# Modulation vectors in unsplit fp32, the vector stationary in four column groups of the array

## The chip, the cores and the metric

The kernel runs on one NeuronCore of a Trainium2 chip. The metric is the device time of one execution in microseconds. The kernel before takes 2354.13 us (median of 3 runs, 2353.49 to 2354.79).

## The reference, cut to what matters

The program is a small diffusion transformer: a first block of two layers, and a second block of two layers, over 256 latent tokens and 256 context tokens of width 1024, all in fp32. Every layer shifts, scales and gates its tokens by modulation vectors, which are the product of one vector (for the latents) or another (for the context) with a wide weight matrix:

```python
shift, scale, gate = jnp.split(jax.nn.silu(c) @ w_mod + b_mod, 3, axis=-1)
shift_c, scale_c, gate_c = jnp.split(jax.nn.silu(c_ctx) @ w_mod + b_mod, 3, axis=-1)
hx = rmsnorm(x, g_pre) * (1 + scale[:, None]) + shift[:, None]
...
q, k, v, ga, uf, gf, zc, bc, cc, gc = split_cols(hx @ w_in, PROJ_SIZES)
...
x_new = x + gate[:, None] * rmsnorm(y, g_post)
```

`w_mod` is 1024 x 3072 for each of the two layers of the first block; the second block has `ada_w_2`, 1024 x 9216 for each of its layers. So each weight matrix of modulation is read once, for two vectors.

## The kernel before

Tokens stand feature-major in SBUF: 128 features on the partitions, 8 such tiles, 512 tokens (256 latent, 256 context) along the free dimension. A projection takes a chunk of 256 weight columns (1 MB, `[128, 8, 256]`), splits it into a high and a low part in fp32r (`wchunk`, lines 161 to 186: ScalarE casts at L184 or, for head chunks, L178, VectorE subtracts at L185 or L179), and forms each product as three fp32r products (`mm3`, L194 to L196). It accumulates over the 8 feature tiles into one of three PSUM banks named `acc` (or two named `sc`); other work uses three banks named `wk`. Raw weights land in two slots `wr`, and some `xr` more (4 in the opening, 1 in the first block); all are loaded by the SP queue. A tile scheduler orders the instructions of each engine by data and priority; casts and norms have a raised priority.

The modulation vectors are made in two ways. Those that are needed late in the second block are made on VectorE (`mods_dve`); the change does not touch them. The others, 9216 columns in all, are made on TensorE by `mods_pe`: 2048 columns of the first layer's `w_mod` in the opening, where everything waits for them; its last 1024 columns and the 3072 of the second layer's in the background of the first layer; and 3072 of `ada_w_2` in the background of the second layer. Background work is a generator that is stepped once between the tiles of a projection (`bg`, called from hooks).

A step of `mods_pe` is one chunk of 256 columns. It is loaded and split as any weight chunk; the stationary operand `cst` holds, for each of the 8 feature tiles, 128 columns of which four are not zero (high and low part of each vector, `set_cst`); and 16 fp32r products of 256 columns (L315, L316) accumulate into a `wk` bank. The first four rows of the result are copied to SBUF (L318). One step later two fp32 products with a 4 x 2 selection matrix (L305) turn them to columns, and VectorE adds the bias (L308):

```python
nc.tensor.matmul(ps[:, 0:256], self.cst[:, k], hi[:, k], start=(k == 0), stop=False)
nc.tensor.matmul(ps[:, 0:256], self.cst[:, k], lo[:, k], start=False, stop=(k == KT - 1))
```

In the opening, `first_block` loads x (transposed by L532), steps `mods_pe` eight times while the statistics of x are taken, and then makes the scale (L328) and the norm tiles of x (`apply_norm`: L408 `nu`, L410 `xh`, L411 `xl`), on which the first projections work (keys and values, then the first head chunk of queries). The context follows. In attention, each query head works with fp32r scores (L683, L684), fp32 transposes (L700) and fp32 products with the values (L706), whose outputs are 64 rows of a bank, one half for each head of a pair. Queries and keys are rotated in place in their bank (`rope`) before they are copied out.

Of the kernel before, what the change touches and what calls it, by code (L numbers as in the profile page):

```python
# [62 lines left out]
def constants():  # L63
# [21 lines left out]
    c["sel4"] = np.array([[1, 0], [1, 0], [0, 1], [0, 1]], f)  # L85
# [38 lines left out]
class Kern:  # L124
# [25 lines left out]
    def rawpool(self, n):  # L150
        """further slots for weights on their way in"""
        from contextlib import contextmanager

        @contextmanager
        def cm():
            with self.tc.tile_pool(name="rx", bufs=1, reuse_waits="tile") as rx:
                self.wx, self.rb, self.nw = (rx if n else None), n, 0
                yield
                self.wx = None
        return cm()  # L160
# [50 lines left out]
    def proj(self, chunk, cols, xs, segs, evict=None, korder=False, alloc=None, hook=None, order=None):  # L211
        """cols: functions (weights, k) -> [P, 128]; xs: (hi, lo) per k; evict(i, psum)"""
# [24 lines left out]
    def proj_first(self, tiles, xs, segs):  # L237
        """tiles: (chunk, column function, evict) triples; one segment after the other"""
        pss = [self.facc() for _ in tiles]
        both = list(zip(pss, tiles))  # L240
        for s in segs:
            # the last segment chunk by chunk, which frees the first one early
# [55 lines left out]
    def mods_pe(self, w, ncols, dst, bias, pin=0):  # L298
        nc = self.nc
        rows = []  # L300

        def columns(ch, row):
            ps2 = self.wk()
            for j in range(2):
                ins = nc.tensor.matmul(ps2[:, 2 * j:2 * j + 2], row[:, j * P:(j + 1) * P], self.sel4[0:4, :], start=True, stop=True)  # L305
                if pin and j == 0:
                    self.tc.keep_in_program_order(ins)
            nc.vector.tensor_tensor(dst[:, :, 2 * ch:2 * ch + 2], ps2[:, 0:4].rearrange("p (f v) -> p v f", v=2),  # L308
                                    bias[:, None, 2 * ch:2 * ch + 2].to_broadcast([P, 2, 2]), ALU.add)

        for ch in range(ncols // 256):
            hi, lo = self.wcols(w, ch * 256)
            ps = self.wk()
            for k in range(KT):
                nc.tensor.matmul(ps[:, 0:256], self.cst[:, k], hi[:, k], start=(k == 0), stop=False)  # L315
                nc.tensor.matmul(ps[:, 0:256], self.cst[:, k], lo[:, k], start=False, stop=(k == KT - 1))  # L316
            row = self.p1.tile([4, 256], F32, name="mrow", tag="mrow", bufs=3)
            nc.scalar.copy(row, ps[0:4, 0:256])  # L318
            rows.append((ch, row))
            if len(rows) > 1:  # L320
                columns(*rows.pop(0))
            yield
        columns(*rows.pop(0))
        yield
# [25 lines left out]
    class Stat:  # L350
# [19 lines left out]
        def columns(self, pin=False):  # L370
            """1/rms per token, tokens on partitions"""
# [19 lines left out]
        def finish(self, alloc=None, pin=False):  # L391
            """the same on every partition, tokens along the free dimension"""
# [40 lines left out]
    def run(self):  # L433
        with ExitStack() as es:
# [14 lines left out]
            with tc.tile_pool(name="p1", bufs=1) as self.p1:  # L449
# [3 lines left out]
                self.cst = self.p1.tile([P, KT, P], F32R, name="cst")  # L453
                nc.vector.memset(self.cst.bitcast(F32), 0.0)
                self.set_cst(0)
# [6 lines left out]
    def setup(self):  # L462
# [19 lines left out]
        self.sel4 = cp.tile([4, 2], F32, name="sel4")  # L482
        nc.gpsimd.dma_start(self.sel4, C["sel4"])
# [29 lines left out]
    def set_cst(self, base):  # L513
        """stationary columns [c hi, c lo, c_ctx hi, c_ctx lo]"""
        nc = self.nc
        for v in range(2):
            src = self.vec[:, base + v * 8:base + v * 8 + 8]
            hi = self.cst[:, :, 2 * v]
            nc.scalar.copy(hi, src)
            nc.vector.tensor_tensor(self.cst[:, :, 2 * v + 1], src, hi.bitcast(F32), ALU.subtract)  # L520

    def load_T(self, src, dst, stat, load=None, act=0):
        """token-major [256, 1024] in DRAM -> feature-major dst [P, KT, 256]"""
# [17 lines left out]
    def first_block(self):  # L541
# [4 lines left out]
        with self.rawpool(RI):  # L546
            for _ in self.load_T(I["x"][0], self.X, st[0], self.wload):
                pass
            for i, _ in enumerate(self.mods_pe(I["w_mod"][0, :, 0:2048], 2048, self.m1[0][:, :, 0:16], V["bmod"][:, 0:16],
                                               PM)):  # L550
# [7 lines left out]
        bga = self.mods_pe(I["w_mod"][0, :, 2048:3072], 1024, self.m1[0][:, :, 16:24], V["bmod"][:, 16:24])  # L558
        bgb = self.mods_pe(I["w_mod"][1], 3072, self.m1[1], V["bmod"][:, 24:48])

        def ada():
            self.set_cst(32)
            yield from self.mods_pe(I["ada_w_2"][0, :, 0:3072], 3072, self.m2[0][:, :, 0:24], V["adab0"][:, 0:24])
# [14 lines left out]
    def fb_layer(self, l, stats, bga, bgb, AB):  # L578
# [28 lines left out]
        # a head's queries and keys: [hi; lo] against [hi; hi], and hi against lo  # L607
# [40 lines left out]
        def softmax(pss, width, E, h):  # L648
            """rows of the two query tiles; E <- normalised weights"""
# [141 lines left out]
        if l == 0:  # L791
            # the segments apart: the tiles of x are ready before those of the context
# [16 lines left out]
        else:  # L809
            # x first, its statistics come before the context's  # L810
# [51 lines left out]
        # merge  # L862
# [6 lines left out]
        # out projection and post norm  # L869
# [40 lines left out]
    def second_block(self):  # L910
# [36 lines left out]
        with tc.tile_pool(name="fin", bufs=1, reuse_waits="tile") as fp:  # L947
            # tokens end up on partitions, so that 1/rms goes in last
# [128 lines left out]
    def tokproj(self, chunk, xn, tts, evict):  # L1077
        """token-major product: out[tokens, 256 columns]"""
# [678 lines left out]
```

## Time and profile before

| what | value |
|---|---|
| median of 3 runs | 2354.13 us (2353.49 to 2354.79) |
| span of the profiled execution | 2352.5 us |
| TensorE products, busy | 2287.0 us (97%), 13429 records |
| weight loads of TensorE, busy | 1968.5 us (84%) |
| VectorE, busy | 1631.1 us (69%) |
| ScalarE, busy | 969.5 us (41%) |
| data moved | 327.31 MB, 139 GB/s over the span |
| share of the last chain: TensorE | 53%, and 24% issue |

The profiled execution's own time is its span, 2352.5 us; the median of the runs stands 1.6 us above it. TensorE's products are pipelined: a product's duration reaches past the start of the next one, so that the distance between two starts, not the duration, is what a product takes of the engine. An fp32 product runs as two passes and leaves two records in the trace, an fp32r product one.

### The profile page before, as it was taken

To read this page: it belongs to the slowest core of one execution; us is meant where nothing else is said; L and a number is where in the kernel's file an instruction comes from. 1 tells how busy PE (TensorE), PEld (TensorE's weight loads), DVE (VectorE), ACT (ScalarE), POOL (GpSimd) and SP (SyncE) were. 2 spreads that over 40 slices of the span, in tenths; PEclk is the share of its full clock that TensorE was granted. 3 is DMA by queue.
4 is the path that set the end of the run, shared out by engine and by line. 5 is a ranking of instruction groups with operands and counts; after the bars stand their busy time and mean duration, and the time that the engine had idled before them with its cause. 6 is when DMAs were issued, how large, how long until landed. Compare 5 with 4: busy or idle time off the path is not lost.

```text
span 2352.5 us, 33979 instructions
## 1 busy us (share of the span) xinstructions
PE 2287.0 (97%) x13429; PEld 1968.5 (84%) x13429; DVE 1631.1 (69%) x3445; ACT 969.5 (41%) x1751; POOL 50.5 (2%) x112
## 2 busy tenths in 40 slices
PE   7999988999999999999999999999999999999998
PEld 7777788789888889876798888898888897778998
DVE  7756668768699977667768953376949655646555
ACT  6644555665322224544542222243212235634444
POOL 1000000000000001000000000000000000000000
PEclk9999999999999999999999999999999999999999
DMA  9234435454566633311244632254637433123553
GB/s 292 91 108 141 131 109 182 151 147 161 162 197 197 211 118 96 108 43 48 77 144 137 206 123 90 81 166 143 198 125 254 153 118 102 37 90 126 196 181 126
DMA packets 329935, 327.31 MB, mean 139 GB/s; under 512 B 9292, under 2 KB 327812, under 8 KB 329776
## 3 DMA queue, kind: packets, MB, share of 16 engines
q1 hardware_dynamic: 326688, 321.16, 42.9%
q8 instruction: 105, 1.72, 0.3%
q10 hardware_dynamic: 1952, 2.29, 0.3%
q0 software_dynamic: 1136, 1.70, 0.2%
q14 instruction: 54, 0.44, 0.1%
HBM read 324.07 MB, written 1.05 MB: 138 GB/s over the span
## 4 chain that ended last, share of the span: by engine, by line
PE 53%; issue 24%; DVE 3%; ACT 1%; POOL 0%; POOLq 0%; DVEq 0%; ACTq 0%
PE acc L194 9%; PE acc L195 9%; PE acc L196 9%; PE sc L194 5%; PE sc L195 5%; PE sc L196 5%; PE acc L1087 1%; PE acc L1089 1%; PE acc L1088 1%; DVE wl L185 1%; PE sc L1398 1%; PE wk L1341 1%; PE wk L706 1%; PE sc L1643 1%; PE wk L1646 1%
## 5 line engine op out<-in xcount | busy, mean ns | idle before, releaser
L184 ACT CAST wh<-wr 128x1024 fp32r<-128x1024 f32 (+1 forms) x432 | 423.8, 1026 | 575.3 <-PE acc L195 269.8
L194 PE MATMUL acc<-xh,wh 128*128 128x256 f32 (+1 forms) x1792 | 610.0, 342 | 6.0 <-ACT xh L410 2.2
L196 PE MATMUL acc<-xh,wl 128*128 128x256 f32 (+1 forms) x1792 | 606.1, 339 | 6.4 <-DVE wl L185 6.2
L195 PE MATMUL acc<-xl,wh 128*128 128x256 f32 (+1 forms) x1792 | 606.1, 339 | 1.5 <-DVE xl L411 1.4
L185 DVE TENSOR_TENSOR wl<-wr,wh 128x1024 fp32r<-128x1024 f32 (+1 forms) x432 | 499.5, 1193 | 152.1 <-ACT wh L184 150.0
L194 PEld LDWEIGHTS acc<-xh,wh 128*128 128x128 f32 x1792 | 341.6, 191 | 51.8 <-issue 10.4
L196 PEld LDWEIGHTS acc<-xh,wl 128*128 128x128 f32 x1792 | 342.1, 191 | 44.1 <-DVE wl L185 8.3
L195 PEld LDWEIGHTS acc<-xl,wh 128*128 128x128 f32 x1792 | 342.8, 191 | 40.2 <-issue 5.4
L284 DVE SCALAR_TENSOR_TENSOR macc<-mraw,vec,macc 128x256 f32<-128x256 f32 x728 | 308.9, 475 | 2.4
L194 PE MATMUL sc<-xh,wh 128*128 128x256 f32 (+1 forms) x816 | 272.2, 334 | 7.5 <-ACT xh L410 3.1
L195 PE MATMUL sc<-xl,wh 128*128 128x256 f32 (+1 forms) x816 | 271.3, 333 | 0.0
L196 PE MATMUL sc<-xh,wl 128*128 128x256 f32 (+1 forms) x816 | 271.3, 332 | 0.0
L194 PEld LDWEIGHTS sc<-xh,wh 128*128 128x128 f32 x816 | 156.3, 192 | 22.9 <-ACT xh L410 3.6
L195 PEld LDWEIGHTS sc<-xl,wh 128*128 128x128 f32 x816 | 156.1, 191 | 14.5 <-DVE xl L411 0.2
L196 PEld LDWEIGHTS sc<-xh,wl 128*128 128x128 f32 x816 | 156.1, 191 | 14.0
L194 PE MATMUL acc<-hh,wh 128*128 128x256 f32 (+1 forms) x494 | 164.2, 332 | 0.0
L196 PE MATMUL acc<-hh,wl 128*128 128x256 f32 (+1 forms) x494 | 163.9, 332 | 0.0
L195 PE MATMUL acc<-hl,wh 128*128 128x256 f32 (+1 forms) x494 | 163.9, 332 | 0.0
L1019 ACT CAST hh<-hf 128x512 fp32r<-128x512 f32 (+1 forms) x92 | 50.1, 548 | 207.5 <-DVE hf L1014 207.5
L194 PE MATMUL sc<-hh,wh 128*128 128x256 f32 (+1 forms) x354 | 117.7, 332 | 0.0
L196 PE MATMUL sc<-hh,wl 128*128 128x256 f32 (+1 forms) x354 | 117.4, 332 | 0.0
L195 PE MATMUL sc<-hl,wh 128*128 128x256 f32 (+1 forms) x354 | 117.3, 331 | 0.0
(399 smaller groups left out, 3288.8 us busy)
## 6 DMA issues: line engine op xcount, KB each, us to landing
wr<-in_ffn_w_in_dram SPq DMA_DIRECT2D x92, 1024.0 KB, 5.1
mraw<-in_ada_w_dram SPq DMA_DIRECT2D x60, 1024.0 KB, 5.2
wr<-in_ffn_w_out_dram SPq DMA_DIRECT2D x32, 1024.0 KB, 5.2
wr<-in_ffn_w_out_dram SPq DMA_DIRECT2D x22, 768.0 KB, 4.3
xr<-in_w_mod_dram SPq DMA_DIRECT2D x14, 1024.0 KB, 6.1
wr<-in_even_w_in_dram SPq DMA_DIRECT2D x12, 1024.0 KB, 5.3
wr<-in_odd_w_in_dram SPq DMA_DIRECT2D x12, 1024.0 KB, 5.3
wr<-in_w_mod_dram SPq DMA_DIRECT2D x10, 1024.0 KB, 5.8
```

The lines of the kernel that those rows point to most:

```text
L184: nc.scalar.copy(hi[:, a:b], raw[:, a:b])
L185: nc.vector.tensor_tensor(lo[:, a:b], raw[:, a:b], hi[:, a:b].bitcast(F32), ALU.subtract)
L194: mm(ps, wh, xh, start=start, stop=False)
L195: mm(ps, wh, xl, start=False, stop=False)
L196: mm(ps, wl, xh, start=False, stop=stop)
L284: nc.vector.scalar_tensor_tensor(a, raw[:, k], cs[:, v * 8 + k:v * 8 + k + 1], a, ALU.mult, ALU.add)
L706: nc.tensor.matmul(pso[r, seg], vtok[:, jj, 64 * hh:64 * hh + 64], PT[:, j, :], start=(j == 0), stop=(j == nk - 1))
L1019: nc.scalar.copy(h[0][:, sl], hf)
L1087: mm(o, xn[k][0][:, s], hi[:, k, :], start=(k == 0), stop=False)
L1088: mm(o, xn[k][0][:, s], lo[:, k, :], start=False, stop=False)
L1089: mm(o, xn[k][1][:, s], hi[:, k, :], start=False, stop=(k == KT - 1))
L1341: mm(po[:, dr * 130:dr * 130 + 130], Es[dr][:, sl_, b_ * P:(b_ + 1) * P], V1[:, kt_, hh], start=(n_ == 0), stop=(n_ == len(L) - 1))
```

## The change

`mods_pe` no longer splits the weights. It takes them as blocks of rows: with 2048 columns a block is 128 rows (`[128, 1, 2048]`, 8 KB per row), with 1024 columns two blocks of 128 rows (`[128, 2, 1024]`); either is 1 MB and lands in a raw slot as before. The stationary operand is the unsplit vector pair, 32 columns of which two are not zero. Four products in fp32 send the four quarters of a block's columns to four groups of 32 rows of one `acc` bank, which lie in four column groups of the array. The sum over the 8 feature tiles runs over 8 steps (or 4), during which the bank is held. At the end all 128 rows are copied to SBUF, turned by 4 (or 2) transposes, and the bias is added by one instruction per vector. The stationary operand of the second block's vectors has a tile of its own, so it is filled at the start. The rest of the diff takes out comments (so line numbers shift: `mm3` stands at L193 to L195, the casts at L183 and L184, `set_cst` at L518 and L520).

```diff
-    def mods_pe(self, w, ncols, dst, bias, pin=0):
+    def mods_pe(self, w, ncols, dst, bias, vec, pin=0):
         nc = self.nc
...
-        for ch in range(ncols // 256):
-            hi, lo = self.wcols(w, ch * 256)
-            ps = self.wk()
-            for k in range(KT):
-                nc.tensor.matmul(ps[:, 0:256], self.cst[:, k], hi[:, k], start=(k == 0), stop=False)
-                nc.tensor.matmul(ps[:, 0:256], self.cst[:, k], lo[:, k], start=False, stop=(k == KT - 1))
-            row = self.p1.tile([4, 256], F32, name="mrow", tag="mrow", bufs=3)
-            nc.scalar.copy(row, ps[0:4, 0:256])
-            rows.append((ch, row))
-            if len(rows) > 1:
-                columns(*rows.pop(0))
-            yield
-        columns(*rows.pop(0))
-        yield
+        c0 = 0
+        while c0 < ncols:
+            cw = min(512, (ncols - c0) // 4)
+            kk = 2048 // (4 * cw)
+            nq = cw // P
+            ps = self.acc()
+            for k0 in range(0, KT, kk):
+                raw = self.wload([P, kk, 4 * cw])
+                nc.sync.dma_start(raw, w[k0 * P:(k0 + kk) * P, c0:c0 + 4 * cw].rearrange("(k p) c -> p k c", p=P))
+                for k in range(k0, k0 + kk):
+                    for j in range(4):
+                        ins = nc.tensor.matmul(ps[32 * j:32 * j + 32, 0:cw], vec[:, k], raw[:, k - k0, j * cw:(j + 1) * cw],
+                                               start=(k == 0), stop=(k == KT - 1))
+                        if pin and j == 0:
+                            self.tc.keep_in_program_order(ins)
+                if k0 + kk < KT:
+                    yield
+            row = self.p1.tile([P, 512], F32, name="mrow", tag="mrow", bufs=2)[:, 0:cw]
+            nc.scalar.copy(row, ps[:, 0:cw])
             ps2 = self.wk()
+            for q in range(nq):
+                nc.tensor.transpose(ps2[:, q * P:(q + 1) * P], row[:, q * P:(q + 1) * P], self.ident)
+            f = slice(c0 // P, (c0 + 4 * cw) // P)
+            got = ps2[:, 0:cw].rearrange("p (q j v) -> p j q v", q=nq, j=4)
+            for v in range(2):
+                nc.vector.tensor_tensor(dst[:, v, f].rearrange("p (j q) -> p j q", j=4), got[:, :, :, v],
+                                        bias[:, f].rearrange("p (j q) -> p j q", j=4), ALU.add)
+            c0 += 4 * cw
             yield
...
     def set_cst(self, base):
         nc = self.nc
+        t = self.p1.tile([P, KT, 32], F32, name=f"cst{base}")
+        nc.gpsimd.memset(t, 0.0)
         for v in range(2):
-            src = self.vec[:, base + v * 8:base + v * 8 + 8]
-            hi = self.cst[:, :, 2 * v]
-            nc.scalar.copy(hi, src)
-            nc.vector.tensor_tensor(self.cst[:, :, 2 * v + 1], src, hi.bitcast(F32), ALU.subtract)
+            nc.vector.tensor_copy(t[:, :, v], self.vec[:, base + v * 8:base + v * 8 + 8])
+        return t
...
-                self.cst = self.p1.tile([P, KT, P], F32R, name="cst")
-                nc.vector.memset(self.cst.bitcast(F32), 0.0)
-                self.set_cst(0)
+                self.cst = self.set_cst(0)
```

On TensorE, the end of the opening's modulation and the first projection (`sc` and `acc` from `xh`, `xl`) stand so before; the last product of the last chunk, then the selections of the last two chunks:

```order
L316 MATMUL wk_454<-wl_449,cst_132 128x256
L305 MATMUL wk_473<-sel4_93,mrow_428 128x2 x2
L305 MATMUL wk_477<-sel4_93,mrow_471 128x2 x2
L194 MATMUL sc_626<-xh0_111,wh_493 128x256
L194 MATMUL acc_627<-xh0_111,wh_493 128x256
L195 MATMUL sc_626<-xl0_112,wh_493 128x256
```

In the changed kernel the same place holds the last six blocks of rows, each from its own raw slot, and the transposes:

```order
L312 MATMUL acc_190<-xr_209,cst0_130 32x512 x4
L312 MATMUL acc_190<-xr_215,cst0_130 32x512 x4
L312 MATMUL acc_190<-wr_242,cst0_130 32x512 x4
L312 MATMUL acc_190<-wr_248,cst0_130 32x512 x4
L312 MATMUL acc_190<-xr_254,cst0_130 32x512 x4
L312 MATMUL acc_190<-xr_272,cst0_130 32x512 x4
L322 MATMUL wk_280<-ident_89,mrow_278 128x128 x4
L193 MATMUL sc_432<-xh0_109,wh_299 128x256
L193 MATMUL acc_433<-xh0_109,wh_299 128x256
```

All blocks go to one bank, `acc_190`; the columns are turned once, behind the last of them.

In the first layer, a background chunk before ends between attention's products with the values (`PT`, `vtok`) and a projection tile (`acc_1216`):

```order
L315 MATMUL wk_1193<-wh_1187,cst_132 128x256
L706 MATMUL wk_990<-PT_1174,vtok_547 64x256 x2
L316 MATMUL wk_1193<-wl_1188,cst_132 128x256
L305 MATMUL wk_1212<-sel4_93,mrow_1113 128x2 x2
L194 MATMUL acc_1216<-xh5_121,wh_1121 128x512
L195 MATMUL acc_1216<-xl5_122,wh_1121 128x512
```

In the changed kernel a background step of 2048 columns stands so (`ident`, `E`: attention's transposes; `four`: the Fourier product):

```order
L701 MATMUL wk_1163<-ident_89,E_1076 128x128 x4
L701 MATMUL wk_1169<-ident_89,E_1076 128x128 x4
L312 MATMUL acc_1111<-wr_1179,cst0_130 32x512 x2
L707 MATMUL wk_1110<-PT_1162,vtok_353 64x256 x4
L312 MATMUL acc_1111<-wr_1179,cst0_130 32x512 x2
L755 MATMUL wk_1186<-four_337,uf0_364 128x256
```

The four products of one block are parted two and two by attention's products. Of the 28 background steps eleven are parted in such a way, five of them with blocks of 2048 columns; in the others the four (or eight) stand together.

## Rows read from the trace of the kernel before

**Rows 1.** Part 1 of the page: the span.

```profile
span 2352.5 us, 33979 instructions
```

**Rows 2.** Stretches: length; busy PE, PEld, DVE, ACT, POOL; PEclk, DMA, GB/s.

```profile
60.00:300.00 240.00, 235.73 (x1213) 182.36 (x1214) 153.70 (x328) 130.12 (x261) 0.31 (x1) 0.99 0.38 116
300.00:515.00 215.00, 198.42 (x1339) 174.60 (x1338) 158.39 (x351) 122.52 (x244) 4.09 (x12) 0.95 0.48 145
```

**Rows 3.** Waits of PE, 60 to 515 us: total us, times, longest.

```profile
PE acc L194 <- ACT wh L178: 2.1, 1, 2.1
PE sc L194 <- ACT wh L178: 1.6, 1, 1.6
PE wk L315 <- ACT wh L184: 1.3, 1, 1.3
```

**Rows 4.** Groups by line, 60 to 515 us: busy us, mean ns, idle before.

```profile
L315 PE MATMUL wk<-wh,cst 128*128 128x256 f32 x224 | 58.8, 298 | 1.8 <-ACT wh L184 1.3 <-ACT PT L701 0.5
L316 PE MATMUL wk<-wl,cst 128*128 128x256 f32 x224 | 56.8, 289 | 0.0
L305 PE MATMUL wk<-sel,mrow 4*128 4x2 f32 x112 | 17.3, 255 | 0.5 <-ACT mrow L318 0.5
```

**Rows 5.** Timeline of PE, 100 to 106 us: start, us, line, tiles, shape, count.

```profile
100.82 0.39 PE L195 MATMUL acc<-xl,wh 128*128 128x512 f32 x1
101.05 0.40 PE L196 MATMUL acc<-xh,wl 128*128 128x512 f32 x1
101.37 1.73 PE L706 MATMUL wk<-PT,vtok 128*64 128x256 f32 x7
101.37 0.86 PE L706 MATMUL wk<-PT,vtok 128*64 128x256 f32 x3
102.93 0.38 PE L706 MATMUL wk<-PT,vtok 128*64 128x256 f32 x1
103.24 0.39 PE L315 MATMUL wk<-wh,cst 128*128 128x256 f32 x1
...
105.88 0.50 PE L683 MATMUL sc<-kh,qs 128*128 128x512 f32 x1
```

**Rows 6.** Timeline of PE: fp32 passes alone and in pairs of groups.

```profile
977.14 1.88 PE L1289 MATMUL wk<-R,ident 128*128 128x512 f32 x4
1052.87 1.02 PE L1289 MATMUL wk<-R,ident 128*128 128x512 f32 x2
1039.65 1.12 PE L1398 MATMUL sc<-dqk 64*128 64x512 f32 x2
1083.21 1.13 PE L1398 MATMUL sc<-dqk 64*128 64x512 f32 x4
2030.15 0.65 PE L1643 MATMUL sc<-S,qe 128*64 128x256 f32 x2
2067.53 1.08 PE L1643 MATMUL sc<-S,qe 128*64 128x256 f32 x6
```

**Rows 7.** Timeline of PE: fp32 transposes of 128 columns.

```profile
116.69 0.60 PE L700 MATMUL wk<-ident,E 128*128 128x128 f32 x4
```

**Rows 8.** Stretches of the opening, columns as in rows 2.

```profile
5.00:7.00 2.00, 0.00 (x0) 0.00 (x0) 0.45 (x3) 0.30 (x2) 1.41 (x3) 1.00 0.94 375
12.00:33.00 21.00, 19.27 (x127) 17.27 (x127) 18.61 (x32) 17.39 (x26) 1.26 (x10) 0.92 1.10 347
39.00:41.00 2.00, 0.60 (x4) 0.52 (x4) 1.97 (x8) 0.62 (x1) 0.00 (x0) 1.00 1.03 403
```

**Rows 9.** Timeline of ACT, DVE and PE behind the last landing.

```profile
33.71 2.00 ACT L184 CAST wh<-xr 128x1024 fp32r<-128x1024 f32 x2 [0.26 <-DMA xr<-in_w_mod_dram]
...
40.56 0.87 DVE L408 SCALAR_TENSOR_TENSOR nu<-X,A,sc 128x256 f32<-128x256 f32 x2
...
41.63 0.58 PE L194 MATMUL sc<-xh,wh 128*128 128x256 f32 x1 [1.99 <-ACT xh L410]
```

**Rows 10.** Groups by line, ACT, 0 to 60 us.

```profile
L534 ACT COPY C<-wk 128x512 f32<-128x512 f32 x4 | 2.2, 592 | 2.6 <-issue 1.3 <-PE wk L532 1.3
```

More of the change, by code (lines that the diff above doesn't have):

```diff
@@ L84, in constants @@
     c["sel"] = sel.reshape(P, 4 * P)
-    c["sel4"] = np.array([[1, 0], [1, 0], [0, 1], [0, 1]], f)
     ch = np.arange(64)
@@ L296, in mods_dve @@
         yield
-    def mods_pe(self, w, ncols, dst, bias, pin=0):
+    def mods_pe(self, w, ncols, dst, bias, vec, pin=0):
         nc = self.nc
-        rows = []
-        def columns(ch, row):
-            ps2 = self.wk()
[L304 to L309, printed above, removed]
-        for ch in range(ncols // 256):
-            hi, lo = self.wcols(w, ch * 256)
-            ps = self.wk()
-            for k in range(KT):
-                nc.tensor.matmul(ps[:, 0:256], self.cst[:, k], hi[:, k], start=(k == 0), stop=False)
-                nc.tensor.matmul(ps[:, 0:256], self.cst[:, k], lo[:, k], start=False, stop=(k == KT - 1))
-            row = self.p1.tile([4, 256], F32, name="mrow", tag="mrow", bufs=3)
-            nc.scalar.copy(row, ps[0:4, 0:256])
-            rows.append((ch, row))
-            if len(rows) > 1:
-                columns(*rows.pop(0))
@@ L481, in setup @@
         nc.sync.dma_start(self.ident, C["ident"])
-        self.sel4 = cp.tile([4, 2], F32, name="sel4")
-        nc.gpsimd.dma_start(self.sel4, C["sel4"])
         self.ones = cp.tile([P, P], F32, name="ones")
@@ L549, in first_block @@
             for i, _ in enumerate(self.mods_pe(I["w_mod"][0, :, 0:2048], 2048, self.m1[0][:, :, 0:16], V["bmod"][:, 0:16],
-                                               PM)):
+                                               self.cst, PM)):
                 if i == 0:
@@ L557, in first_block @@
         st[0] = rbx
-        bga = self.mods_pe(I["w_mod"][0, :, 2048:3072], 1024, self.m1[0][:, :, 16:24], V["bmod"][:, 16:24])
-        bgb = self.mods_pe(I["w_mod"][1], 3072, self.m1[1], V["bmod"][:, 24:48])
+        bga = self.mods_pe(I["w_mod"][0, :, 2048:3072], 1024, self.m1[0][:, :, 16:24], V["bmod"][:, 16:24], self.cst)
+        bgb = self.mods_pe(I["w_mod"][1], 3072, self.m1[1], V["bmod"][:, 24:48], self.cst)
         def ada():
-            self.set_cst(32)
-            yield from self.mods_pe(I["ada_w_2"][0, :, 0:3072], 3072, self.m2[0][:, :, 0:24], V["adab0"][:, 0:24])
+            cst = self.set_cst(32)
+            yield from self.mods_pe(I["ada_w_2"][0, :, 0:3072], 3072, self.m2[0][:, :, 0:24], V["adab0"][:, 0:24], cst)
         bgc = ada()
```

## The prediction

> **What bounds the kernel now.** I read the page first (a span of 2352.5 us [rows 1]), then the busy time by stretch, then TensorE's waits, then the spacing of single products. The modulation products that change stand in three places: 8 chunks of 256 columns in the opening 40 us, 16 in the first layer (60 to 300 us) and 12 in the second (300 to 515). In the second place TensorE is busy 235.7 of 240 us, in the third 198.4 of 215, while the DMA engines are used to 0.38 and 0.48 [rows 2]. So behind 60 us TensorE's own time ends last, and what is taken out of its queue shortens the run almost one to one. Its waits there are few, the longest for hi/lo casts [rows 3]. The opening is another thing: at 12 to 33 us the DMA engines run at their limit, 347 GB/s [rows 8], and a cast waits for each landing [rows 9].
>
> **What goes.** A background chunk is 16 one-pass products (224 and 224 records for 28 chunks) and two fp32 selections that run as two passes each (112 records) [rows 4]. The reader is to see in the timeline that products overlap, so that their price is the distance from start to start, not the duration: the chunk that starts at 103.24 us lets the next work start at 105.88, 2.64 us later, its first 0.1 us being the way out of the product before it [rows 5]. I take 2.55 (2.45 to 2.64) x 28 = 71.4 us of TensorE. With it go two casts of 1.0 us on ScalarE [rows 9] and as many subtractions on VectorE per chunk.
>
> **What comes.** 28 pieces of 1 MB: 16 of one block of 128 rows by 2048 columns (four products of 512 columns) and 12 of two blocks by 1024 (eight products of 256). Each is unsplit fp32, so two passes. A pass costs 0.43 us for 512 columns (four passes in 1.88 us, two in 1.02) [rows 6] and 0.22 for 256 (seven in 1.73, three in 0.86) [rows 5]. The four products of a block write different column groups of the array, and all hangs on whether they run at once. No row shows four groups of 32. The nearest rows show two. In rows, four passes of 512 columns take 1.13 us where two alone take 1.12. In columns, two passes of 256 take 0.65 us and a run of six, of which two pairs lie in different column groups, takes 1.08 instead of the 0.65 + 4 x 0.22 = 1.5 of a queue [rows 6]. So a second group was free. The bounds for four groups are then 2 passes' time per block (all at once), 4 (two at a time) and 8 (one after the other); I take 2, as the rows nearest to it lost nothing.
>
> The Trainium skill (TensorE: Matmul & The Clock Gate, section Measured speedup vs the span model) speaks against this: it gives 2.38 for three column tiles, not 3. At that share per group my passes would take a quarter longer, an estimate of 6 us more for the sum below. The pairs of this trace show no such loss; no run here shows three.
>
> Entering and leaving the grouped mode costs too: from a 512-column product to a 64-column group 0.32 us instead of 0.23, and back 0.31 instead of 0.22 [rows 5]. With 0.05 for the first weights (two passes of one group last 0.65 [rows 6], not 0.22 + 0.38) I take 0.23 per visit (0.18 to 0.3). A piece of either kind is then about 2 x 0.43 + 0.23 or 4 x 0.22 + 0.23 = 1.1 us: 16 x 1.09 + 12 x 1.11 = 30.7. The turn of the rows adds 14 fp32 transposes, 28 passes at 0.11 to 0.15 (four in 0.60) [rows 7]: 3.6. The order tears eleven pieces apart, with attention products in between: five of the 512-column kind pay a second 0.86 + 0.23, six of the other 0.43 + 0.23, together 9.4. Sum 43.7; TensorE gains 71.4 - 43.7 = 27.7 us.
>
> **The opening.** Eight pieces of 1 MB are 8.39 MB: 24.2 us at 347 GB/s. The rows of x and of the context, 4 KB long, came at 375 and 403 GB/s [rows 8]; the new rows are 8 KB, so at 403 they take 20.8, 3.4 us less. TensorE needs 0.9 us per piece against 2.6 us of transfer, so it hides. Behind the last landing there were 7.9 us to the first projection product (33.71 to 41.63) [rows 9]. Now there are one block (0.96), a copy of 512 columns (0.59 [rows 10]), four transposes (0.9), two additions (0.35), the scale (0.24), the first norm tile (1.07, as 40.56 to 41.63 [rows 9]) and some 0.6 of hand-overs: 4.7, so 3.2 less. Of the 6.6 us the next thing takes a part back: the first projection's casts land at the same time and now stand between the norm tiles on VectorE, 2.4 us that lay ahead of them before. I take 5 (2 to 7).
>
> The Trainium skill (DMA: Bandwidth & Descriptors, section Where 436 GB/s comes from) sets about 358 GB/s as the limit of loads from HBM; by it the transfers gain 0.8 us instead of 3.4. The 403 of this trace is above it, so I keep the measured rate.
>
> **The rest.** The casts' relief: TensorE's longest waits for casts behind 60 us that the chunks' own casts can have held up are 2.1, 1.6 and 1.3 [rows 3]; I take 2.5 (0 to 5), since other casts stay. Against it: a sum now holds one of the three `acc` banks over 4 or 8 steps, where a chunk held a `wk` bank for one. The projections between go on with two banks; a bank is emptied by one copy (0.59 [rows 10]) while the next tile's 24 products run for 5 us, but a rotated query tile stays longer: 2.4 us lost (0 to 10). A piece also stays in its raw slot until its product; before it, the early split freed the slot. The transfer share of 0.38 leaves room, I cost it at nothing. The stationary's memset and copies move to the start of POOL's and VectorE's queues, where TensorE waits for x anyway: nothing.
>
> Sum: 27.7 + 5 + 2.5 - 2.4 = 32.8 us off the span of 2352.5. The median stands 1.6 us above it (2354.13), so 2321.3.
>
> **The rivals.**
> - Two groups at a time. Pieces cost 4 or 8 passes: 16 x 1.95 + 12 x 1.99 = 55.1, and the torn pieces lose only the visit, 2.5; with 3.6 that is 61.2, a gain of 10.2. With the opening: 2339. For it: two is all the trace shows, and four unsplit streams ask for twice the data of a pair.
> - One after the other, the slower side. The four groups queue: 16 x 3.67 + 12 x 3.75 = 103.7, + 3.6 + 2.5 = 109.8, 38.4 more than before; in the opening eight blocks of 3.44 us outlast the transfers, 1 us lost: 2393. It decides from about 5.3 passes' time per block, where a piece costs 2.5 us and eats the opening's gain too. Against it: the pair of column groups in [rows 6].
> - The bank. If each of the 28 pieces made a projection tile wait for a copy, 0.6 us x 28 = 17 come back: 2338. For it: rotated tiles are long in their bank; against: 5 us per tile to empty one.
> - Another engine is the bound behind 60 us, VectorE and ScalarE with the softmax. Then the opening alone stays: 2349. For it: 17 us of idle TensorE in the third place; against: 4 of 240 in the second, and both engines are relieved as well.
>
> **How the numbers follow.** Forecast 0.70 (its own range 2309 to 2333), two at a time 0.10, bank 0.04, other engine 0.05, one after the other 0.11. About 0.2% (5 us) is what a measurement can tell from no change. Faster is all but the last case and a little of the fourth: 0.86; same 0.03; slower 0.11. The range reaches from 2308 (no torn piece matters, all relief comes) to 2345, past the pairs and the bank, and leaves out the queue.
>
> **What would show it.** In the trace of the changed kernel the four products of a block start within some 0.05 us and their second passes 0.43 us later; a piece takes 1.1 us from its start to the next work's; 3.4 us or more between them is the queue, 1.9 the pairs. The first projection product starts at 35 to 37 us. GB/s at 12 to 28 us is near 400. No projection product waits for an `acc` copy. The prediction is wrong if the stretch to the end of the second layer is not some 28 to 38 us shorter, or if anything behind it moves.

## The result and the profile after

The changed kernel takes 2316.26 us (median of 4 runs, 2314.59 to 2319.22), the kernel before 2353.84 beside it (4 runs). The ratio is 0.9839, 95% interval 0.9825 to 0.9853: faster by 37.6 us, where 32.8 were forecast. The execution whose trace is read here is the slowest of the four, 2319.22 us; its span, 2317.4 us, leaves out 1.8 us of it. The time of an execution is thus not its span, and the 1.6 us between median and span of the kernel before need not be a difference between two executions.

The head of the page, and the busy time by stretch (columns: stretch, us; then busy us and instructions of PE, PEld, DVE, ACT, POOL; granted clock; DMA share; GB/s):

```profile
span 2317.4 us, 33109 instructions
PE 2243.0 (97%) x13111; PEld 1893.1 (82%) x13111; DVE 1546.5 (67%) x3348; ACT 892.0 (38%) x1645; POOL 50.3 (2%) x113
60.00:285.00 225.00, 216.89 (x1091) 148.43 (x1090) 114.02 (x282) 93.17 (x208) 0.71 (x9) 0.99 0.39 125
285.00:500.00 215.00, 201.50 (x1404) 167.98 (x1404) 148.64 (x355) 113.47 (x246) 5.43 (x6) 0.97 0.54 164
```

The last two lines are the first and second layer, which [rows 2] showed. TensorE is still the fullest engine in both. The forecast can't be judged from these shares: that the same work ends earlier shows only when the same product is looked for in both traces. The kernel has 10,368 projection products (`mm3`) in both; I number them by their start. The table gives the start of the n-th in the kernel before and, for the other kernels, how much later (+) or earlier (-) it starts, all from the profiled executions, so that a column can stand some 3 us from the median of its kernel (the scheduler also swaps neighbours, so a single row in the middle of a layer is good to a few us; n = 0, 96, 1056, 1536 and the last are the clean marks: first product, context half, start and end of the second layer's work, end):

```
n      before  changed  opening  backgr.  casts  VectorE  no casts
       (us)             only     only     back   work     in before
0        41.6    -7.7    -7.0      0.2    -7.7    -6.9      0.3
96       60.9    -4.6    -3.9      1.1    -4.9    -3.0      0.4
672     301.1   -16.5    -3.6    -11.7   -14.7   -12.1      2.5
1056    361.8   -11.9    -3.6     -8.5   -11.4    -9.3      4.2
1536    518.7   -37.3    -3.6    -33.3   -23.5   -15.9    -10.0
last   2342.6   -35.2    -3.7    -33.1   -19.3   -13.6     -9.9
```

In the column of the changed kernel, 4.6 us come from the opening, 7.3 from the first layer and 25.4 from the second. That is not where the work went: 16 of the 28 pieces lie in the first layer. The last columns are experiments, below.

### The profile page after: what moved, and what is told of

It reads as the page before. It is cut to its first block, busy times and chain, and to the rows that moved or that the text cites. A ratio compares the mean times of both kernels' runs of the same rounds, so it can differ in the third digit from the quotient of the medians.

```text
span 2317.4 us, 33109 instructions
## 1 busy us (share of the span) xinstructions
PE 2243.0 (97%) x13111; PEld 1893.1 (82%) x13111; DVE 1546.5 (67%) x3348; ACT 892.0 (38%) x1645; POOL 50.3 (2%) x113
## 4 chain that ended last, share of the span: by engine, by line
PE 50%; issue 40%; DVE 5%; ACT 2%; DMA 2%; POOL 1%; SPq 0%; POOLq 0%; DVEq 0%; ACTq 0%
PE acc L193 9%; PE acc L194 9%; PE acc L195 8%; PE sc L193 3%; PE sc L194 3%; PE sc L195 3%; PE wk L707 2%; DVE wl L184 2%; PE acc L312 1%; PE acc L1088 1%; PE acc L1090 1%; PE acc L1089 1%; DMA wr<-in_w_in_dram 1%; PE wk L701 1%; PE sc L1399 1%
## 5 line engine op out<-in xcount | busy, mean ns | idle before, releaser
L193 PE MATMUL acc<-xh,wh 128*128 128x256 f32 (+1 forms) x1792 | 613.1, 343 | 14.5 <-DVE qs L644 4.9
L195 PE MATMUL acc<-xh,wl 128*128 128x256 f32 (+1 forms) x1792 | 606.5, 339 | 5.5 <-DVE wl L184 5.4
L183 ACT CAST wh<-wr 128x1024 fp32r<-128x1024 f32 (+1 forms) x394 | 385.9, 1024 | 559.0 <-PE acc L194 261.6
L184 DVE TENSOR_TENSOR wl<-wr,wh 128x1024 fp32r<-128x1024 f32 (+1 forms) x394 | 455.3, 1192 | 159.1 <-ACT wh L183 157.1
L193 PEld LDWEIGHTS acc<-xh,wh 128*128 128x128 f32 x1792 | 343.4, 192 | 73.0 <-issue 24.5
L195 PEld LDWEIGHTS acc<-xh,wl 128*128 128x128 f32 x1792 | 343.9, 192 | 42.8 <-DVE wl L184 6.4
L193 PE MATMUL sc<-xh,wh 128*128 128x256 f32 (+1 forms) x816 | 272.0, 334 | 6.8 <-ACT xh L415 4.0
L195 PE MATMUL sc<-xh,wl 128*128 128x256 f32 (+1 forms) x816 | 270.9, 332 | 0.0
L193 PEld LDWEIGHTS sc<-xh,wh 128*128 128x128 f32 x816 | 156.1, 191 | 22.7 <-ACT xh L415 4.7
L195 PEld LDWEIGHTS sc<-xh,wl 128*128 128x128 f32 x816 | 155.7, 191 | 14.2 <-DVE wl L178 0.2
L193 PE MATMUL acc<-hh,wh 128*128 128x256 f32 (+1 forms) x494 | 164.1, 332 | 0.0
L195 PE MATMUL acc<-hh,wl 128*128 128x256 f32 (+1 forms) x494 | 163.9, 332 | 0.0
L193 PE MATMUL sc<-hh,wh 128*128 128x256 f32 (+1 forms) x354 | 117.6, 332 | 0.0
L195 PE MATMUL sc<-hh,wl 128*128 128x256 f32 (+1 forms) x354 | 117.4, 332 | 0.0
```

Of the source, the lines that this page charges most:

```text
L183: nc.scalar.copy(hi[:, a:b], raw[:, a:b])
L184: nc.vector.tensor_tensor(lo[:, a:b], raw[:, a:b], hi[:, a:b].bitcast(F32), ALU.subtract)
L193: mm(ps, wh, xh, start=start, stop=False)
L195: mm(ps, wl, xh, start=False, stop=stop)
```

## The experiments

**Do the four groups run at once?** Two kernels that send the products to other column groups (line 312):

```diff
- ps[32 * j:32 * j + 32, 0:cw] ... start=(k == 0), stop=(k == KT - 1)
# queue
+ ps[32 * (k % 4):32 * (k % 4) + 32, 0:cw] ... start=(k < 4 and j == 0), stop=(k >= 4 and j == 3)
# pairs
+ ps[64 * (k % 2) + 32 * (j % 2):..., 0:cw] ... start=(k < 2 and j < 2), stop=(k >= 6 and j >= 2)
```

> All four products of a block of 128 rows write the same column group (the group changes with the block), so that they queue; the same number of products, bytes, copies and transposes, the sums themselves are mixed up. If the gain is the four groups running at once, a block costs eight passes in place of two: 6 x 0.43 = 2.6 us more for each of the 28 background pieces, 73 us, and in the opening a block (3.4 us) outlasts its transfer (2.5 us), some 7 us: 2316 + 80 = 2396 (2380 to 2410), and products of a block start 0.43 to 0.86 us apart. If the gain came from the casts taken off ScalarE and VectorE and from freed buffers rather than from TensorE's queue, most of it stays: 2340 or less.

> The four products of a block write two column groups in turn (a, b, a, b), so that two run at once and not four; the sums are mixed up. If time is the number of passes that follow each other, a block costs four passes in place of two: 0.86 us more x 28 = 24, the opening hides it: 2316 + 24 = 2340 (2335 to 2345). If turning from group to group costs something of its own, or a pair runs no better than one, it comes nearer to the queue of the first experiment (2396). If a quarter is lost between two and four groups already, the difference to the changed kernel is under 18 us.

Queue: 2366.55 us, ratio to before 1.005 (1.0035 to 1.0065), 50.3 us more than the changed kernel. Pairs: 2332.17 (2328.29 to 2337.49), 0.9908 (0.9892 to 0.9924), 15.9 more. Both lie below the ranges expected. TensorE's timeline (start, length, line, tiles, shape, count), a whole piece of 512 columns and one of 256 in the changed kernel, with the work before or behind:

```profile
121.59 0.66 PE L701 MATMUL wk<-ident,E 128*128 128x128 f32 x4
122.17 1.07 PE L312 MATMUL acc<-xr,cst 128*32 128x512 f32 x8
123.17 0.50 PE L193 MATMUL acc<-xh,wh 128*128 128x512 f32 x1
222.03 1.07 PE L312 MATMUL acc<-xr,cst 128*32 128x256 f32 x16
223.03 0.50 PE L193 MATMUL acc<-xh,wh 128*128 128x512 f32 x1
```

The same two in the pairs:

```profile
120.61 1.91 PE L312 MATMUL acc<-xr,cst 128*32 128x512 f32 x8
122.45 0.50 PE L193 MATMUL acc<-xh,wh 128*128 128x512 f32 x1
224.65 1.08 PE L312 MATMUL acc<-xr,cst 128*32 128x256 f32 x16
225.66 0.50 PE L193 MATMUL acc<-xh,wh 128*128 128x512 f32 x1
```

And in the queue:

```profile
128.13 3.62 PE L312 MATMUL acc<-xr,cst 128*32 128x512 f32 x8
131.68 0.49 PE L193 MATMUL acc<-xh,wh 128*128 128x512 f32 x1
115.36 2.81 PE L312 MATMUL acc<-wr,cst 128*32 128x256 f32 x16
118.09 0.50 PE L193 MATMUL acc<-xh,wh 128*128 128x512 f32 x1
```

The reader is to take the distance from the piece's start to the next work's: 1.00, 1.84 and 3.55 us for 512 columns, so 0.85 more for each further two passes in a row, and nothing is lost from two groups to four (where a piece is torn so that one product of it stands alone, that takes 0.98 as well). For two blocks of 256 columns it is 1.00, 1.01 and 2.74. There the pairs lose nothing, since the two blocks of a piece lie in different groups and overlap; in the queue they overlap in part. That is why both came out below their expectations (2340 and 2396): pairs cost 16 x 0.85 = 13.6 and not 24, the queue 16 x 2.55 + 12 x 1.74 = 62 and not 73, less what a torn piece costs in the changed kernel already (two visits of 0.98). The pairs' expectation read a difference of under 18 us as a loss between two and four groups; the distances rule that out. Summed over the background, the distances of `L312` grow by 47.7 us in the queue (43.8 to 91.6) and the time by 50.3, of which 3.8 lie in the opening (the 96th product): what is put into TensorE's queue is paid nearly one to one. In the pairs they grow by 10.9 us (to 54.7) and the time by 15.9, with runs that spread over 9 us.

**The two places apart.** In the first kernel the new product stands in the opening alone, in the second in the background alone; the other place keeps the split product of before. To find room, the new product's stationary operand and rows (in the first kernel) or the old one's (in the second) lie in buffers that are idle then.

```diff
# opening only
- bga = self.mods_pe(...)   bgb = self.mods_pe(...)   yield from self.mods_pe(...)
+ bga = self.mods_old(...)  bgb = self.mods_old(...)  yield from self.mods_old(...)
# background only
- enumerate(self.mods_pe(I["w_mod"][0, :, 0:2048], ...
+ enumerate(self.mods_old(I["w_mod"][0, :, 0:2048], ...
```

> The new product in the opening alone, the split one-pass product as before in the background (60 to 515 us). The opening's first projection product came 7.7 us earlier in the changed kernel, and 4.3 us of it were left at 70 us. If that part is kept to the end: before - 4 to 5 = 2349 (2346 to 2351). If the first layer's casts and waits take it back: 2353, no change from before. If the opening were worth its whole 7.7 us: 2346.

> The new product in the background alone, the split one in the opening. If the two parts add up, this lacks what the opening gave: 2316 + 4 to 5 = 2321 (2318 to 2324), of it about 8 us gained in the first layer and 25 in the second. If the first layer gave only 8 us because the opening's gain had left it waiting for casts, it gives more here and the total is nearer to 2317.

Opening only: 2350.24, 0.9982 (0.9972 to 0.9991), 4.5 us off before's 2354.79. Background only: 2320.82, 0.9852 (0.9835 to 0.9868), 34.0 off. They add up (38.5 against 37.6), and the table shows that the opening's 3.6 us stay to the end, while the background alone also gives 8.5 us at the start of the second layer and 25 in it.

**The rows of the opening's transfers.**

```diff
- nc.sync.dma_start(raw, w[...].rearrange("(k p) c -> p k c", p=P))
+ if pin:   # opening: every second 256 columns in one transfer, the others in a second
+     for b in range(2):
+         half = lambda t: t[:, 0].rearrange("p (a b c) -> p a b c", b=2, c=256)[:, :, b]
+         nc.sync.dma_start(half(raw), half(src))
```

> Only the opening's eight pieces are fetched in rows of 1 KB (two transfers per piece with every second 256 columns) in place of 8 KB; same bytes, same products. If the length of the rows sets the rate, the eight pieces take 24.2 us (347 GB/s) in place of 20.6 (407): the first projection product starts some 3.5 us later (37.5 in place of 34.0 us), and some 2 to 3.5 us of it are left at the end: 2318.5 to 2320. If the rate came from the order of the transfers or from fewer casts beside them: no change, near 400 GB/s.

2318.74 us, 0.9848 (0.9834 to 0.9861). The time alone (2.5 us more than the changed kernel, intervals that overlap) would not settle it; the trace does. A piece is two transfers here and not one, but before the change one transfer of 1 MB in rows of 1 KB came no faster. The stretch from 12 to 28 us, the changed kernel first (last number GB/s):

```profile
12.00:28.00 16.00, 10.71 (x70) 3.46 (x69) 4.64 (x18) 2.66 (x8) 1.30 (x10) 0.89 1.01 413
```

```profile
12.00:28.00 16.00, 11.46 (x62) 3.47 (x61) 4.61 (x18) 2.63 (x8) 1.29 (x10) 0.79 1.10 347
```

347 GB/s is what [rows 8] showed before the change. The opening's end, again the changed kernel first (in brackets the idle time and what ended it):

```profile
28.66 1.06 PE L312 MATMUL acc<-xr,cst 128*32 128x512 f32 x8 [1.44 <-DMA xr<-in_w_mod_dram]
30.43 0.66 PE L322 MATMUL wk<-ident,mrow 128*128 128x128 f32 x4 [0.71 <-ACT mrow L319]
33.98 0.58 PE L193 MATMUL sc<-xh,wh 128*128 128x256 f32 x1 [2.89 <-ACT xh L415]
```

```profile
32.60 1.94 PE L318 MATMUL acc<-xr,cst 128*32 128x512 f32 x8 [1.84 <-DMA xr<-in_w_mod_dram]
37.88 0.58 PE L193 MATMUL sc<-xh,wh 128*128 128x256 f32 x1 [1.53 <-ACT xh L421]
```

With 1 KB rows the last block starts 3.9 us later, and so does the first projection product. So half of the opening's 7.7 us are the rate, half the shorter tail.

**The held `acc` bank.**

```diff
- ps = self.acc()
+ ps = self.wk()
```

> The sum of a piece is kept in a wk bank and not in one of the three acc banks; nothing else is edited (the order of TensorE's background moves a little with it). In the changed kernel two projection tiles wait for an acc bank that a rotated query tile still holds (gaps of 3.2 us at 79 and 2.7 us at 383 us). If these waits are a loss, they go and the time falls by 3 to 6 us: 2311 (2309 to 2314). If the attention's transposes, which share the wk banks, then wait in their place: no change or up to 5 us slower.

2316.79 us, 0.9839 (0.9826 to 0.9853): no change. TensorE's waits from 60 to 500 us (total, times, longest), the changed kernel and this one:

```profile
PE acc L195 <- DVE wl L184: 5.4, 2, 5.0
PE acc L193 <- DVE qs L644: 4.9, 2, 2.9
PE acc L193 <- ACT wh L177: 3.8, 1, 3.8
PE acc L193 <- ACT wh L183: 2.8, 2, 2.2
```

```profile
PE acc L195 <- DVE wl L184: 6.0, 3, 5.0
PE acc L193 <- ACT wh L183: 4.1, 3, 2.3
PE acc L193 <- ACT wh L177: 2.5, 1, 2.5
PE sc L193 <- ACT wh L177: 2.3, 1, 2.3
```

The bank's 4.9 us (`qs L644` empties the bank) are gone, and waits for casts grew from 3.8 + 2.8 to 4.1 + 2.5 + 2.3. So the bank wait seems to have lain ahead of a cast that was late as well.

**The torn pieces.** The expectation speaks of the first product of each block; the edit pins all four products of every block to program order, also in the background:

```diff
- if pin and j == 0:
+ if True:
```

> The first product of each block is pinned to program order in the background too, so that no piece is torn by attention products. The changed kernel makes 39 visits to the grouped mode for 28 pieces; a whole piece takes 1.0 us and a visit's two halves 2 x 0.98 (512 columns) or 0.56 + 0.99 (256). Eleven torn pieces would then give back 7 us: 2309 (2307 to 2312). If the torn pieces fill time in which TensorE would wait for a softmax, or the pinned ones wait for their own transfer: no change or slower, up to 5 us.

2328.65 us, 0.9893 (0.9878 to 0.9908): 12.4 us slower, the second case of the forecast but more than twice its 5 us. All 28 pieces are whole now, most of 1.0 us, and the distances of `L312` fall from 43.8 to 36.6 us: 7.2 us of TensorE came back, as expected. But two places in its timeline show what the pieces had been doing:

```profile
123.36 0.66 PE L701 MATMUL wk<-ident,E 128*128 128x128 f32 x4
127.19 1.08 PE L707 MATMUL wk<-PT,vtok 128*64 128x256 f32 x2 [3.17 <-DVE sft L654]
223.90 0.66 PE L701 MATMUL wk<-ident,E 128*128 128x128 f32 x4
228.54 1.08 PE L707 MATMUL wk<-PT,vtok 128*64 128x256 f32 x2 [3.99 <-DVE sft L655]
```

TensorE stands idle until VectorE's softmax steps are done, 12.0 us in five such waits of `L707` (none of any size in the changed kernel). So the waits cost more than the whole pieces gave. The two traces differ by 6.4 us at the last product, the medians by 12.4, so the size is good to some 6 us.

It is not the tearing that covered the two longest of these waits. In the changed kernel the same places hold a whole piece, and ten or twelve projection products behind it (the lines at 121.59 to 123.17 and 222.03 under the first experiment). What the pin takes away is the place: of the 24 stretches from a transpose of attention to its next product with the values, 18 hold modulation products in the changed kernel, none in this one, where they often stand behind the values. The torn pieces do the same with their halves, at the place of the other three waits and, with nothing else between, as here:

```profile
132.18 1.05 PE L312 MATMUL acc<-wr,cst 128*32 128x512 f32 x4
133.16 1.94 PE L707 MATMUL wk<-PT,vtok 128*64 128x256 f32 x8
135.03 1.05 PE L312 MATMUL acc<-wr,cst 128*32 128x512 f32 x4
```

**What the removed casts were worth.** Four kernels. The first casts and subtracts each background piece into the hi/lo buffers, unread; the second takes the buffers but casts one column; the third does the engines' work into a scratch and leaves the buffers alone; the fourth is the third without ScalarE's part (both also keep one `mrow` tile in place of two, to make room for the scratch). The code is shortened:

```diff
+ pin or self.relief(raw, kk, cw)          # behind a piece's products
+ def relief(self, raw, kk, cw):
+     hi, lo = self.wsplit([P, kk, 4 * cw])                        # 1, 2
+     for h in range(2):                                           # 1; in 2 one column of hi and lo
+         nc.scalar.copy(hi[:, :, b], raw[:, :, b])
+         nc.vector.tensor_tensor(lo[:, :, b], raw[:, :, b], hi[:, :, b].bitcast(F32), ALU.subtract)
+     for h in range(4): nc.scalar.copy(dh, r[:, h * 512:(h + 1) * 512])         # 3
+     for h in range(8): nc.vector.tensor_tensor(dl, b, b, ALU.subtract)         # 3, 4 (256 columns)
```

> The changed kernel, and each of the 28 background pieces is also cast and subtracted in two halves into the hi/lo buffers, as the chunks of before were; nothing reads these. It prices what the removed casts gave. If their relief is the 2.5 us (0 to 5) of the forecast: 2319 (2316 to 2321). The second layer gained 25 us where TensorE's products there became only 16.6 us shorter; if the other 8 came from ScalarE, VectorE and the hi/lo buffers being free, this costs 8 us or more: 2325.

> As the experiment that added the casts back (18 us slower than the changed kernel), but only one column of each piece is cast and subtracted: the hi/lo buffers are taken in turn as before, ScalarE and VectorE have next to nothing to do. If the removed casts helped by leaving the two hi/lo buffers to the projections: 2326 or more (half of the 18 us and up). If they helped by their engine time: 2317 (2315 to 2319).

> The other half: the casts' engine time without their buffers. Each background piece is copied on ScalarE (4 x 512 columns) and subtracted on VectorE (8 x 256 columns) into a small scratch that nothing reads; the hi/lo buffers are left alone, and VectorE doesn't wait for ScalarE. If engine time is what the change gave back: 2326 or more. If it was the buffers: 2317 to 2319. If both come out small, the 18 us of the full casts are the order that the work then took and not a price.

> Of the engine time that was added back (16.5 us slower than the changed kernel) only VectorE's part: eight subtractions of 256 columns per background piece into a scratch, no copies on ScalarE. In the second layer VectorE is the fuller of the two (34.8 of 40 us at 380 to 420 us before the change, ScalarE 25.4). If VectorE alone is what TensorE waited for there: 2331 (2328 to 2334). If ScalarE, which stands ahead of VectorE in every cast and softmax: 2318 or less. If both have a part: 2322 to 2327.

Casts back: 2334.53 us, 0.9915 (0.9903 to 0.9928), 18.3 slower than the changed kernel. Buffers alone: 2314.53, 0.9832 (0.9819 to 0.9846), nothing. Engine time alone: 2332.84, 0.9911 (0.9897 to 0.9924), 16.6 slower. VectorE's part alone: 2339.86, 0.9928 (0.9914 to 0.9941, before at 2355.50 on that chip), 23.6 slower, above the range of all three cases. So VectorE's work, with the raw slots that it holds, is enough for the whole effect. That it costs 7 us more without ScalarE's copies than with them is not explained: these sizes hold to some 7 us, and the order that the work takes is a part of them. In the second layer VectorE is busy 29.7 us more than in the changed kernel, where the full casts add 23.8. In the table VectorE's part costs 1 us in the first layer (6.3 gained in place of 7.3) and 18.8 in the second (6.6 in place of 25.4).

Two things these four do not part. The added work holds each raw slot until its last subtraction: in the second layer SP waits 81.3 us for it with the engine time back (`SPq L309 <- DVE dl L1736: 47.0` and `SPq L168 <- DVE dl L1736: 34.3`), and TensorE waits 5.0 us for modulation weights, 1.7 in the changed kernel. So a part of the price may be late transfers and not VectorE's queue. And the second kernel frees its hi/lo buffers after one column, while before the change a chunk held them until its products were done (ScalarE's casts waited 36.4 us for `L315`, 60 to 515 us); what that holding cost is not tested by itself.

And the other way round, the kernel before with the casts of the background taken out:

```diff
- hi, lo = self.wcols(w, ch * 256)      # 16 products of 256 columns, one pass
+ raw = self.wload([P, KT, 256])        # 8 products of 128 columns, two passes
+ nc.tensor.matmul(ps[:, c], self.cst[:, k].bitcast(F32), raw[:, k, c], ...)   # c: half of the columns
```

> The kernel before, with the background chunks read unsplit: no casts, and to keep TensorE's time the same only half of the columns of each block are multiplied (8 products of 128 columns in two passes each in place of 16 of 256 in one; half of the products is left out). Opening as before. If the casts' relief adds to the product's gain: before less 18 = 2336. If it is worth something only once TensorE's queue is shorter: 2350 to 2354. The forecast's 2.5 us would be 2351.5.

2344.28 us, 0.9956 (0.9942 to 0.9969): 9.8 us faster than before, between the two cases of the forecast. TensorE's time was not kept quite the same: the products start 0.112 us apart and not 0.120, which over 448 is 3.6 us. So the casts, with the buffers that they held, are worth 6 to 10 us there, and some 18 in the changed kernel. The second layer shows why. The stretch is that of its work (n = 1056 to 1536), in the order before, no casts in before, changed, buffers alone, casts back, engine time back, VectorE's part back (columns as in the first profile above: PE is the first busy time, DVE the third, the clock stands behind POOL's):

```profile
361.80:518.70 156.90, 147.42 (x943) 124.58 (x941) 122.17 (x267) 97.84 (x193) 1.60 (x1) 0.96 0.51 153
366.00:508.70 142.70, 140.69 (x943) 118.76 (x941) 94.45 (x243) 76.10 (x169) 1.07 (x1) 1.00 0.56 168
349.90:481.40 131.50, 127.39 (x836) 95.67 (x835) 93.77 (x235) 72.58 (x159) 1.07 (x1) 0.99 0.59 182
346.30:483.40 137.10, 133.09 (x837) 97.20 (x835) 94.04 (x247) 74.06 (x171) 1.07 (x1) 0.98 0.56 174
350.40:495.20 144.80, 132.30 (x836) 97.90 (x835) 117.52 (x254) 96.52 (x179) 1.61 (x1) 0.95 0.55 169
345.70:492.20 146.50, 133.94 (x840) 99.12 (x838) 123.12 (x327) 99.59 (x203) 2.40 (x3) 0.94 0.56 175
352.50:502.80 150.30, 137.51 (x840) 99.28 (x838) 123.48 (x327) 74.58 (x159) 1.77 (x2) 0.94 0.53 165
```

With the work on VectorE (first and last three lines) TensorE stands idle for 9.5 to 12.8 us of the stretch, and its mean granted clock is 0.94 to 0.96; without it 2.0 to 4.1 us and 0.98 to 1.00. So TensorE pays twice: it waits, and it is slower for some time after the wait (an example stands in the next section). Before the change the casts' removal takes 14.2 us from the stretch: 7.5 are idle time, and the clock, 0.96 of the full one over 157 us, is by an estimate the other 6 to 7. In the changed kernel the same casts cost 13.3. So in the second layer they are worth much the same in either order; what differs is the first layer, where the kernel before loses 3.8 us without its casts, and the end.

Over the whole stretch VectorE is busy 78% before. It is fuller in a part of it:

```profile
380.00:420.00 40.00, 34.11 (x183) 29.27 (x184) 34.83 (x75) 25.41 (x49) 0.00 (x0) 0.87 0.49 158
```

There VectorE, at 87%, is fuller than TensorE. With VectorE's part back the chain of waits runs for the most part over VectorE from 378.7 to 399.5 us. That VectorE bounds this part before the change too is argued and not shown: TensorE's longest waits there are for ScalarE's casts [rows 3], and one of these casts waited 4.4 us of the 40 for a buffer that `L315` still read.

## Why the prediction was right

The time (2321.3 forecast, 2316.3 measured) and its sign came out, and the mechanism that all hung on is shown: the starts of a block's four products lie 6 to 7 ns apart in the records, the second passes 0.43 us later, a piece takes 1.00 us where 1.1 was predicted. The stretch to the end of the second layer is 37.3 us shorter (28 to 38). But that the sum came within 5 us is partly luck: two terms were off in opposite directions.

- **TensorE's gain (27.7 us).** Mis-sized as a share of the time. By the distances from start to start, TensorE's modulation products behind 60 us fell from 79.9 to 45.6 us, 34.3: more than I had, since before's chunks also held 3.9 us of waits and stood in part at the lower clock. But with VectorE's work as it was, the background gained only about 15 (casts back against before, 19.8 us, less the opening's 4.5). Taken after the casts it is 23 to 27 (37.6 less the casts' 6 to 10 and the opening's 4.5).
- **The casts' relief (2.5 us, 0 to 5).** This step failed: 6 to 10 us out of the kernel before, some 18 put back into the changed one. I priced it at half of the waits that name a cast [rows 3]. In the second layer all of TensorE's idle time fell, from 9.5 to 2.0 us without the casts, and I had no term for the lower clock behind the waits, 6 to 7 us. The mean of a 215 us stretch [rows 2] hid the 40 us in which VectorE is at 87%. The rival "another engine is the bound" had this much in it for the second layer; its price was wrong, because this change relieves just that engine.
- **The torn pieces (9.4 us of loss).** About right as TensorE's own time (7.2), but pinning the pieces doesn't get it back. It costs 12.4 us, since the pieces, torn or whole, also cover waits for softmax; I had no term for that.
- **The bank (2.4 us of loss; no projection product waits for `acc`).** Two do, 4.9 us together, and taking the wait away gives nothing.
- **The opening (5, 2 to 7).** 4.5 measured by itself. The first projection product came at 33.98 (35 to 37 predicted): 413 GB/s (near 400), 3.9 us for the rows (3.4). So the 347 GB/s that I took for the DMA engines' limit [rows 8] was what rows of 1 KB reach. What it lost again by 60 us is 3.1 us where 1.6 were forecast, by the cause named there: casts and norm tiles land together. ScalarE's first norm tile, ready after 31.53 + 0.4 us on VectorE, stood behind the cast of the first weights:

```profile
32.47 1.04 ACT L183 CAST wh<-wr 128x1024 fp32r<-128x1024 f32 x1 [2.10 <-DMA wr<-in_w_in_dram]
33.42 0.50 ACT L415 ACTIVATE xh<-nu,m 128x256 fp32r<-128x256 f32 x1
```

- **The raw slot (nothing).** Not nothing. The chain of waits at the end of the first layer (start, length, step):

```profile
256.45 0.60 PE acc L312 x6
...
257.07 0.37 SPq L168
...
257.48 6.89 DMA wr<-in_w_in_dram
...
264.40 0.63 ACT wh L177
...
265.07 0.50 PE acc L193
```

A piece's products end at 257.05, which frees its slot; SP asks for the next weights at once, they land 6.9 us later, and TensorE has waited 3.8 us for their cast. It is read from the chain and not tried by itself.
- **What is late next.** I named nothing for the first layer's end, where the table steps back from -16.5 to -11.9 (the background alone from -11.7 to -8.5). TensorE reaches the output projection earlier, and its weights are not there: the chain has their transfer, `282.88 8.74 DMA wr<-in_w_out_dram`, then the cast. The products around that wait:

```profile
290.11 0.28 PE L194 MATMUL sc<-xl,wh 128*128 128x256 f32 x1
290.23 0.28 PE L195 MATMUL sc<-xh,wl 128*128 128x256 f32 x1
292.74 0.50 PE L193 MATMUL acc<-xh,wh 128*128 128x256 f32 x1 [2.23 <-ACT wh L183]
...
294.59 0.41 PE L194 MATMUL acc<-xl,wh 128*128 128x256 f32 x1
294.81 0.41 PE L195 MATMUL acc<-xh,wl 128*128 128x256 f32 x1
```

Ahead of it they start 0.12 us apart, behind it 0.21 until 296.3 us, where the granted clock is 0.53 on the mean (292.7 to 296.3; 1.00 ahead of the wait and behind this stretch; so for most of it the lower level, 1.2 GHz): a wait of 2.2 us costs some 1.5 to 2 us more, an estimate from the two distances.
- **Nothing behind the second layer moves.** 2.1 us do in this profile (-37.3 to -35.2). With the casts or the engine time put back it is 4.2 and 3.8, with the buffers alone 1.3 the other way, without casts in before 0.1, and none of these edits touches that part. I take it for the scatter of single executions, which in the runs of one kernel is up to 9 us; no run shows its cause.

The rivals: the queue and the pairs were built and are slower by 50 and 16 us than what the chip does, where I had 72 and 18 (2393 and 2339 against 2321).

## What to carry to other kernels

Do not price elementwise work that goes away by the waits that name it alone. Look at how full its engine is in the worst stretch of the stage, and at the clock after the waits: here two casts and two subtractions per chunk, on engines that were not the fullest of their stage on the mean, were worth 6 to 18 us. A small independent product that the scheduler moves about and tears apart may be the filler of another engine's latency; look at what waits where it stands before pinning it. And unsplit fp32 with a narrow stationary operand in four column groups costs no more than one group alone, which saves the split as well as the passes.

## What the runs showed of the hardware

- Column groups overlap beyond one block: in the queue, where each block's eight passes go one after the other, the next block in another group began before the last was through (the second block of a piece 0.89 us behind the first, whose passes start 0.22 us apart), and 16 passes of 256 columns took 2.74 us where the eight of 512 took 3.55.
- Four unsplit fp32 streams at once lose nothing against two: two blocks of 256 columns took 1.00 us by four groups and 1.01 by pairs in turn. The Trainium skill (TensorE: Matmul & The Clock Gate, section Measured speedup vs the span model) gives 2.38 for three column tiles; no run here shows three, and the four of this trace show no such loss.
- The same bytes came at 413 GB/s in rows of 8 KB and at 347 in rows of 1 KB, in pieces of 1 MB (before the change) or in halves of them. The Trainium skill (DMA: Bandwidth & Descriptors, section Where 436 GB/s comes from) sets about 358 GB/s as the limit of loads from HBM; the 413 of this trace is above it.
